# Block 0 of an in-projection: first casts interleaved by quarters, raw weights in x's raw buffers, rotation's sum on VectorE

## The chip, the cores and the metric

One core of one Trainium2 chip runs the kernel, with its engines TensorE (PE; its weight loads are shown as PEld), VectorE (DVE), ScalarE (ACT), GpSimd (POOL) and SyncE (SP, whose queue, SPq, issues the transfers). The metric is device microseconds of one execution, the median of several runs; lower is better.

## The reference

One layer of a hybrid encoder over 2048 prompt tokens and 8 x 16 sample tokens, all in float32. Cut to what matters here:

```python
def trunk_layer(x, pos, ..., w_in, ...):
    qm, km, vm, om, ip, fp, qa, ka, va = split_in(x @ w_in)
    km = km.reshape(B, T, M_HEADS, M_HEAD_DIM) * (M_HEAD_DIM ** -0.5)
    ...
    hm, C1, n1, m1 = mlstm_chunkwise(qm, km, vm, logi, logf, C0, n0, m0, mchunk)
    og = jax.nn.sigmoid(om)
    qa = rope(qa.reshape(B, T, A_Q_HEADS, A_HEAD_DIM), pos)
    ka = rope(ka.reshape(B, T, A_KV_HEADS, A_HEAD_DIM), pos)
    ha = swa_prompt(qa, ka, va, attn_sinks)      # or swa_step for the sample tokens
    mix = jnp.concatenate([hm, ha], axis=-1) @ w_out
    h = layer_norm(DEEPNORM_ALPHA * x + mix, ln1_g, ln1_b)
    f, conv_rows = conv_ffn(h, conv_prev, w_up, w_conv, b_conv, w_down)
    return layer_norm(DEEPNORM_ALPHA * h + f, ln2_g, ln2_b), ...

def rope(x, pos):
    ...
    return jnp.concatenate([x1 * cos - x2 * sin, x2 * cos + x1 * sin], axis=-1)
```

Only `x @ w_in` for the first 512 prompt tokens and the sample tokens (block 0), and the rotation of `qa` there, are touched by the change.

## The kernel before

**Stages.** The in-projection runs over four blocks of tokens (`IBLOCKS`; block 0 is tokens 0 to 511 and the 128 sample tokens, called the batch). After it, and partly woven into it, come the mLSTM and attention chains, the out-projection, and the ConvFFN.

**Products.** The wide part of `w_in` is cut into five groups of 512 columns (`NG`; groups 0 and 1 are q and k, 2 is qa with the rotation, 3 the output gate with a tanh, 4 is v). Each group is multiplied by a block of x as 2 x 2 quadrants in seven half-size products instead of eight, called steps 1, 2, 7, 6, 5, 4, 3 here; "product 3.5" is group 3, step 5. Steps 1, 2, 3, 4 and 5 use a quadrant of the weight itself or one with a difference in it, steps 7 and 6 sums and differences made in place in the raw weights by DVE (`split_first`, L516, L518, L521, L537). The products accumulate in three PSUM banks A, B, C (`self.ib`, shown as dps): steps 1 and 2 in A, 6, 5 and 3 in B, 7 and 4 in C (L722). A product is 24 matmuls of 128x256; in block 0 steps 1, 2, 5 and 4 have 12 more for the batch (L744, bank psx).

**Operands.** Every float32 operand is split into a rounded part and a remainder: ACT casts the high part (L220 for weights, L580 for x), DVE subtracts it for the low part (L221, L581). TensorE multiplies high x high, high x low and low x high.

**Order of block 0.** `i_begin` writes the order down: products 0.1, 0.2, 1.1, then the narrow gate-and-key tiles (L748, weights `wg`), then 0.7, 0.6, 0.5, 0.4, 0.3, 1.7; then for each group g: g.6, g.2, g.5, (g+1).1, g.4, g.3, (g+1).7; the last group ends 4.6, 4.2, 4.5, 4.3, 4.4. A list of units in the same order says what is loaded (`next_raw`, L429) and split (`next_split`, L475). `advance` runs both as far ahead as room allows: the split weights lie in a ring of four units, so a split waits for the product four units back; the raw weights lie in four slots taken in turn (`raw_slot`, tag wraw), and the next load waits until the oldest slot's weight is used for the last time (`raw_free`, L415). A group loads four raw quadrants, at its steps 1 (a11), 7 (a21), 6 (a22) and 2 (a12). a11 is done after the split of step 2, a21 after that of step 5, a22 after 4, a12 after 3.

Groups 2 to 4 write the split weights of steps 6, 5, 7 and 3 to memory for the later blocks (L533); x's four raw quadrants of a block lie in buffers xr1 to xr4 (`x_load`, L549).

**After a product** (`i_after`, L798): step 6 copies B out (L801), step 5 copies B (L801) and adds C (L807), step 4 adds C to step 6's copy (L807), steps 2 and 3 copy A and B out (L793, or the tanh at L790), step 3 also copies A to B (L829). For group 2 each result is then rotated (`rope`, L888): two products into a buffer rb, one in place (L900) and a sum (L901) that POOL does, for the batch too (`i_batch`); then SP stores it (L783, L840).

**Start.** SP loads x's first quadrant and the first weight in halves, in turn. `split_first` casts and subtracts the weight in four quarters, `x_steps` those of x in four quarters (L576 to L581).

The instructions of each engine run in the order in which a scheduler put them, except that TensorE's order is the program's.

Of the kernel before, what the change touches and what calls it, by code (L numbers as in the profile page):

```python
# [14 lines left out]
P = 128  # L15
# [31 lines left out]
HT = 2 * P  # L47
# [157 lines left out]
class Prog:  # L205
# [137 lines left out]
    def i_begin(self):  # L343
# [40 lines left out]
        self.halves = [0, 0]  # L384
        self.raws = []
        self.raw_of = {}
        self.xn = self.ny = 0
        self.hs = {}
        self.spare = False
# [39 lines left out]
    def next_raw(self):  # L429
# [4 lines left out]

        there = u[0] == "p" and u[1] == 0 and (u[2] == 0 and u[3] != 1 or u[3] in (5, 4, 3) or u[2:] == (1, 1))
        there = there or u[:2] == ("g", -1)
        if not there and not self.kept(u) and not self.raw_free():
            return False
        self.ur += 1
        if u[0] == "p":  # L440
            _, b, g, s = u
            quad = {1: (0, 0), 2: (0, 1), 7: (1, 0), 6: (1, 1), 4: (1, 1)}
            if b == 0:

                if s in (5, 4, 3):
                    return True
                if g == 0:
                    if s == 1:
                        self.i_first_weights()
                    return True  # L450
                if (g, s) == (1, 1):
                    e = self.raw_of[g, quad[s]] = [self.tp.tile([P, 4, HT], F32, name="wraw", tag="qk", bufs=2), False]
                    nc.sync.dma_start(e[0], a["wi"][g][quad[s]])
                    return True
                self.raw_of[g, quad[s]] = e = self.raw_slot([P, 4, HT])
                src = a["wi"][g][quad[s]]
            elif self.kept(u):
                return True
            else:
                self.raw_of[u] = e = self.raw_slot([P, 4, HT])  # L460
                src = a["wi"][g][quad[s]] if s in (1, 2, 4) else self.zws[g][SUMS.index(s)][0]
# [43 lines left out]
    def split_first(self, g, s, hi, lo):  # L505
# [19 lines left out]
        q = {1: a11, 7: a11, 6: a11, 2: a12, 3: a12, 5: a21, 4: a22}[s]  # L525
        n = 4 if (g, s) == (0, 1) else 1
        f = r[q].rearrange("p a b -> p (a b)")
        for i in range(n):
            c = slice(i * 1024 // n, (i + 1) * 1024 // n)
            self.split(hi[:, c], lo[:, c], f[:, c])  # L530
        if g >= KEPT and s in SUMS:
            for i, t in enumerate((hi, lo)):
                nc.sync.dma_start(self.zws[g][SUMS.index(s)][i].rearrange("p a b -> p (a b)"), t.bitcast(F32))  # L533
# [20 lines left out]
    def x_steps(self, b, *steps):  # L554
# [3 lines left out]
        for s in steps:  # L558
# [4 lines left out]
            elif s == "t2":  # L563

                V.tensor_add(self.xt[0], self.xt[0], r(1))
            elif s == "t4":

                V.tensor_sub(r(4), r(3), self.xt[0])
                self.xt[1] = True
            elif s == "t1":  # L570

                V.tensor_sub(r(2), r(2), r(1))
            else:
                x = self.xt[0] if s in (7, 6) else r({1: 1, 2: 3, 3: 4, "b12": 2, 5: 2, 4: 4}[s])

                self.hx[b, s] = h, l = self.x_slot(4 if s == "b12" else s)  # L576
                n = 4 if (b, s) == (0, 1) else 1
                for i in range(n):
                    k = slice(i * 4 // n, (i + 1) * 4 // n)
                    nc.scalar.copy(h[:, k], x[:, k])  # L580
                    V.tensor_sub(l[:, k], x[:, k], h[:, k].bitcast(F32))  # L581

    def x_single(self, *steps):

# [15 lines left out]
    def i_dense(self):  # L600
# [26 lines left out]
        self.rope_load(IBLOCKS[0][2], 2)  # L627
        self.rope_load(NPT, 1)
        self.next_split()
        self.x_steps(0, 1)  # L630
        self.x_single(1)
        self.next_split()
        self.x_steps(0, 2)
# [10 lines left out]
        for item in self.items:  # L644
# [9 lines left out]
            if item[0] == "t":  # L654
# [14 lines left out]
                elif ti == 3 and b or ti == 4:  # L669
                    self.release(4)  # L670
                elif item in begin:
                    self.x_steps(0, *begin[item])
                if ti == 3 and b or ti == 4:
                    self.x_steps(b, 4)
                    if b:
                        self.x_steps(b, 5)
# [108 lines left out]
    def i_out(self, b, g, i, j, src):  # L785
# [6 lines left out]
        elif not i:  # L792
            nc.scalar.copy(ev, src)  # L793
        if g == 2:
            self.rope(ev, IBLOCKS[b][2 * j], 2, nc.gpsimd)
        self.i_store(b, g, i, j, ev)

    def i_after(self, b, g, s):  # L798
# [32 lines left out]
    def i_batch(self, g):  # L831
# [4 lines left out]
        ev = self.zev()  # L836
        if g == 2:
            nc.scalar.copy(ev, ps)
            self.rope(ev, t, 1, nc.gpsimd)
            nc.sync.dma_start(self.zqa[t], ev)  # L840
            return
        if g < 2:
# [1333 lines left out]
```

## Time and profile before

| what | value |
|---|---|
| median of 3 runs | 2326.87 us (2325.21 to 2328.39) |
| the profiled execution | 2326.59 us |
| its span, first to last instruction | 2324.8 us |
| granted TensorE clock, mean | 0.996 |
| block 0 of the in-projection | about the first 163 us |

Times in rows count from the span's start. A timeline row is start, duration, engine, line, operation, output<-input, shape, count, and in brackets how long the engine was idle before and what released it. A chain row is start, duration and what. A wait row is who waited for whom: us in total, times, longest. A window row is the stretch, its length, busy us (and instructions) of PE, PEld, DVE, ACT and POOL, the granted clock of TensorE, the busy share of the DMA engines, and GB/s. A row of groups is line, engine, operation, operands, count, busy us, mean ns of one, and idle time before. A row of transfers has the count, KB each, and median us from issue to landing.

### The profile page before, as it was taken

The page shows a single profiled execution, that of the slowest core. Times are in us where ns is not written, and L with a number is a line of the kernel's source. Part 1 is how long each engine was busy: PE and PEld are TensorE (multiplying, and loading weights), DVE is VectorE, ACT ScalarE, POOL GpSimd, SP SyncE. Part 2 cuts the span into 40 slices and gives each one's busy share as a digit, 9 for nine tenths or more (in the row PEclk, how much of TensorE's full clock was granted, in tenths as well). Part 3 has the DMA queues.
Part 4 walks back from the last instruction along what each step waited for, and adds up shares of the span by engine and source line. Part 5 has one row for each costly group of instructions (what it writes and reads, how often), then busy time and mean ns, then how long its engine had stood idle before and what let it go on. Part 6 is the DMA issues. An engine that isn't in the chain of part 4 may idle for free.

```text
span 2324.8 us, 39933 instructions
## 1 busy us (share of the span) xinstructions
PE 2282.6 (98%) x14425; PEld 2104.6 (91%) x14425; DVE 1801.6 (77%) x3148; ACT 1304.3 (56%) x2465; POOL 244.3 (11%) x298
## 2 busy tenths in 40 slices
PE   9989999999999999999999999999999999999998
PEld 8989988899987777999999999999999988888887
DVE  8677586787678888987888766778766787796897
ACT  5353466676666665655556455556555644554653
POOL 0101101101111221300002000002000000000100
PEclk9999999999999999999999999999999999999999
DMA  7888889889977667787776899887998886756753
GB/s 275 276 309 287 284 294 328 292 279 330 307 254 259 210 212 242 262 321 283 287 272 252 273 319 323 307 309 264 324 298 265 246 284 224 244 197 216 244 189 109
DMA packets 297365, 624.98 MB, mean 269 GB/s; under 512 B 47052, under 2 KB 140240, under 8 KB 297168
## 3 DMA queue, kind: packets, MB, share of 16 engines
q1 hardware_dynamic: 296304, 619.29, 77.8%
q10 hardware_dynamic: 864, 3.15, 0.4%
q8 instruction: 114, 1.87, 0.3%
q14 instruction: 83, 0.68, 0.1%
HBM read 451.78 MB, written 170.56 MB: 268 GB/s over the span
## 4 chain that ended last, share of the span: by engine, by line
PE 78%; DVE 7%; DMA 4%; ACT 2%; issue 2%; SPq 0%; POOL 0%; DVEq 0%; ACTq 0%; POOLq 0%
PE dps L1880 18%; PE fup L1880 18%; PE dps L735 11%; PE dps L2084 6%; PE fht L2084 5%; PE fup L2084 5%; PE dps L225 2%; PE dps L760 2%; PE dps L227 1%; PE dps L226 1%; PE ppo L1371 1%; DVE w L221 1%; PE psc L1322 1%; DMA txy<-wdn 1%; PE ppt L1365 1%
## 5 line engine op out<-in xcount | busy, mean ns | idle before, releaser
L1880 PE MATMUL dps<-hh,uw 128*128 128x384 f32 (+1 forms) x1848 | 477.5, 327 | 5.3 <-DVE u L1913 2.6
L1880 PE MATMUL fup<-hh,uw 128*128 128x384 f32 (+1 forms) x1848 | 476.5, 326 | 0.0
L1928 DVE SCALAR_TENSOR_TENSOR cc<-u,cw,cc 128x768 f32<-128x768 f32 (+1 forms) x264 | 257.8, 978 | 125.1 <-ACT cc L1926 121.7
L1880 PEld LDWEIGHTS dps<-hh,uw 128*128 128x128 f32 x1848 | 329.4, 188 | 7.6 <-DVE u L1913 3.2
L1880 PEld LDWEIGHTS fup<-hh,uw 128*128 128x128 f32 x1848 | 329.4, 188 | 0.0
L1880 PE MATMUL fup<-hl,uw 128*128 128x384 f32 (+1 forms) x924 | 301.3, 326 | 1.1 <-DVE hl L221 1.1
L1880 PE MATMUL dps<-hl,uw 128*128 128x384 f32 (+1 forms) x924 | 301.0, 326 | 0.0
L735 PE MATMUL dps<-w,oh 128*128 128x256 f32 x1344 | 253.4, 284 | 10.1 <-ACT zev L801 5.4
L221 DVE TENSOR_TENSOR w<-wraw,w 128x1024 fp32r<-128x1024 f32 (+2 forms) x163 | 187.9, 1158 | 61.9 <-ACT w L220 59.5
L735 PEld LDWEIGHTS dps<-w,oh 128*128 128x128 f32 x1344 | 211.4, 190 | 23.1 <-issue 9.8
L220 ACT CAST w<-wraw 128x1024 fp32r<-128x1024 f32 (+2 forms) x163 | 161.1, 995 | 124.4 <-PE dps L735 52.2
L220 ACT CAST uw<-wraw 128x1024 fp32r<-128x1024 f32 x126 | 123.3, 982 | 173.7 <-PE dps L2084 104.2
L221 DVE TENSOR_TENSOR uw<-wraw,uw 128x1024 fp32r<-128x1024 f32 x126 | 142.6, 1132 | 63.9 <-ACT uw L220 63.8
L735 PE MATMUL dps<-w,ol 128*128 128x256 f32 x672 | 187.3, 279 | 0.0
L1926 ACT ACTIVATE cc<-u,cw 128x768 f32<-128x768 f32 (+1 forms) x132 | 132.0, 1000 | 96.5 <-DVE u L1922 93.3
L735 PE MATMUL dps<-oh,w 128*128 128x256 f32 x896 | 171.4, 285 | 4.9 <-ACT oh L580 1.7
L1880 PEld LDWEIGHTS fup<-hl,uw 128*128 128x128 f32 x924 | 173.5, 188 | 1.9 <-DVE hl L221 1.9
L1880 PEld LDWEIGHTS dps<-hl,uw 128*128 128x128 f32 x924 | 173.5, 188 | 0.0
L2084 PE MATMUL fup<-uw,fu 128*128 128x512 f32 x726 | 169.0, 389 | 0.0
L2084 PEld LDWEIGHTS fup<-uw,fu 128*128 128x128 f32 x726 | 136.2, 188 | 28.2
L2084 PE MATMUL dps<-uw,fu 128*128 128x512 f32 x660 | 161.0, 389 | 0.1
L735 PEld LDWEIGHTS dps<-oh,w 128*128 128x128 f32 x896 | 141.3, 189 | 11.0 <-issue 4.1
(336 smaller groups left out, 4601.0 us busy)
## 6 DMA issues: line engine op xcount, KB each, us to landing
uw<-zw SPq DMA_DIRECT2D x176, 512.0 KB, 5.1
zw<-uw SPq DMA_DIRECT2D x88, 512.0 KB, 2.9
w<-zws SPq DMA_DIRECT2D x72, 512.0 KB, 6.5
wv<-wup SPq DMA_DIRECT2D x66, 512.0 KB, 6.0
wraw<-wi SPq DMA_DIRECT2D x64, 512.0 KB, 5.0
wraw<-zt SPq DMA_DIRECT2D x60, 512.0 KB, 4.5
wraw<-wdn SPq DMA_DIRECT2D x45, 512.0 KB, 3.8
wraw<-wo SPq DMA_DIRECT2D x40, 512.0 KB, 4.7
```

Of the source, the lines that this page charges most:

```text
L220: nc.scalar.copy(hi, src)
L221: nc.vector.tensor_sub(lo, src, hi.bitcast(F32))
L225: mm(out, ah, bh, start=start, stop=False)
L226: mm(out, ah, bl, start=False, stop=False)
L227: mm(out, al, bh, start=False, stop=stop)
L735: mm(o, l, r, start=s in (1, 7) and c == k == i == 0, stop=k == 3 and i == 2, skip_group_check=True)
L760: mm(o, x, w, start=k == i == 0, stop=k == KD - 1 and i == 2, skip_group_check=True)
L1322: nc.tensor.matmul(ps[kvh][:, j, :nk], q[rs, j0 + j], k[rs, sel], start=i == 0, stop=i == 2)
L1880: mm(ps, l[:, k], r[:, k], start=s in (1, 7) and k == 0 and i == 0, stop=k == 3 and i == 2, skip_group_check=True)
L1926: S.activation(c[:, v], u[:, v, 2:2 + n], AF.Identity, bias=w[3], scale=w[2])
L1928: V.scalar_tensor_tensor(c[:, v], u[:, v, i:i + n], w[i], c[:, v], op0=ALU.mult, op1=ALU.add)
L2084: mm(ps, l[:, k, c], r[:, k], start=s in (1, 4, 7) and u == 0 and k == 0 and i == 0, stop=u == nu - 1 and k == n - 1 and i == 2, skip_grou ...
```

## The change

Three edits in block 0; what is computed stays the same.

1. The eight casts of x's first quadrant and the first weight (a quarter each), and their subtractions, are written as one sequence: x, x, w, w, w, x, w, x, each cast issued after the one before. Before, x's and w's were written apart.
2. Two entries `x_room` let the weights of group 3 for steps 1 and 7 live in x's raw buffers xr1 and xr3, once x of block 0 has been used there (after tile 2), and skip the test for a free slot. x of block 1 goes into the same buffers afterwards.
3. In block 0 the rotation's sum is added by DVE, not POOL.

```diff
+        self.x_room = {1: [None, False], 7: [None, False]}
...
+        room = self.x_room.get(u[3]) if u[0] == "p" and u[1:3] in ((0, 1), (0, 3)) else None
+        there = there or room is not None and room[1]
         if not there and not self.kept(u) and not self.raw_free():
             return False
...
-                self.raw_of[g, quad[s]] = e = self.raw_slot([P, 4, HT])
+                if room and room[1]:
+                    e = self.x_room[s] = [self.x_raw(1 if s == 1 else 3), False]
+                else:
+                    e = self.raw_slot([P, 4, HT])
+                self.raw_of[g, quad[s]] = e
                 src = a["wi"][g][quad[s]]
...
-        for i in range(n):
-            c = slice(i * 1024 // n, (i + 1) * 1024 // n)
-            self.split(hi[:, c], lo[:, c], f[:, c])
+        if n > 1:
+            x = self.xr[0, 1]
+            xh, xl = self.hx[0, 1] = self.x_slot(1)
+            fv, hv, lv = [t.rearrange("p (a b) -> p a b", a=4) for t in (f, hi, lo)]
+            after = None
+            for h, l, src, k in ((xh, xl, x, 0), (xh, xl, x, 1), (hv, lv, fv, 0), (hv, lv, fv, 1),
+                                 (hv, lv, fv, 2), (xh, xl, x, 2), (hv, lv, fv, 3), (xh, xl, x, 3)):
+                with self.tc.issue_after(after) if after else nullcontext():
+                    after = nc.scalar.copy(h[:, k], src[:, k]).ins
+                V.tensor_sub(l[:, k], src[:, k], h[:, k].bitcast(F32))
+        else:
+            self.split(hi, lo, f)
...
-                n = 4 if (b, s) == (0, 1) else 1
-                for i in range(n):
-                    k = slice(i * 4 // n, (i + 1) * 4 // n)
-                    nc.scalar.copy(h[:, k], x[:, k])
-                    V.tensor_sub(l[:, k], x[:, k], h[:, k].bitcast(F32))
+                nc.scalar.copy(h, x)
+                V.tensor_sub(l, x, h.bitcast(F32))
...
-        self.x_steps(0, 1)
...
+                    for e in self.x_room.values() if ti == 2 else ():
+                        e[1] = True
...
-            self.rope(ev, IBLOCKS[b][2 * j], 2, nc.gpsimd)
+            self.rope(ev, IBLOCKS[b][2 * j], 2, nc.gpsimd if b else nc.vector)
...
-            self.rope(ev, t, 1, nc.gpsimd)
+            self.rope(ev, t, 1, nc.vector)
```

What it moves, at three places. First, ACT at the start (xr is x's quadrant, wraw the raw weight, oh and w their high parts; dps<-dps is the copy of A to B after product 0.1). Before:

```order
L580 COPY oh<-xr 128x256
L220 COPY w<-wraw 128x256 x4
L580 COPY oh<-xr 128x256 x3
L592 COPY xs<-xsr 128x512
L220 COPY w<-wraw 128x1024
L580 COPY oh<-xr 128x1024
L592 COPY xs<-xsr 128x512
L809 COPY dps<-dps 128x512
```

Now:

```order
L543 COPY oh<-xr 128x256 x2
L543 COPY w<-wraw 128x256 x3
L543 COPY oh<-xr 128x256
L543 COPY w<-wraw 128x256
L543 COPY oh<-xr 128x256
L605 COPY xs<-xsr 128x512
L220 COPY w<-wraw 128x1024
L823 COPY dps<-dps 128x512
L593 COPY oh<-xr 128x1024
```

x's second quarter stands ahead of all weights, and the copy of A to B has moved ahead of the cast of x's next quadrant. DVE's subtractions follow the same order.

Second, ACT around products 3.6 and 3.5 (numbers are buffers; w_1530, w_1562, w_1592 and w_1639 are the weights of 3.5, 4.1, 3.4 and 3.3; zev_1590 is B copied out after 3.6, zev_1683 after 3.5). Before:

```order
L220 COPY w_1530<-wraw_1224 128x1024
L793 COPY zev_1520<-dps_250 128x512
L829 COPY dps_250<-dps_249 128x512
L220 COPY w_1562<-wraw_1494 128x1024
L801 COPY zev_1590<-dps_250 128x512
L220 COPY w_1592<-wraw_1284 128x1024
L790 ACTIVATE zev_1634<-dps_249 128x512
L220 COPY w_1639<-wraw_1337 128x1024
L801 COPY zev_1683<-dps_250 128x512
```

Now (w_1532 is 3.5's):

```order
L220 COPY w_1532<-xr_1043 128x1024
L807 COPY zev_1522<-dps_250 128x512
L843 COPY dps_250<-dps_249 128x512
L220 COPY w_1562<-wraw_1288 128x1024
L220 COPY w_1592<-wraw_1183 128x1024
L815 COPY zev_1590<-dps_250 128x512
L804 ACTIVATE zev_1634<-dps_249 128x512
L220 COPY w_1639<-wraw_1228 128x1024
L815 COPY zev_1683<-dps_250 128x512
```

The casts for 4.1 and 3.4 both stand ahead of the copy of B now. On DVE, group 3's first operations on the raw weights (xr_1041 is a11, xr_1043 a21, wraw_1183 a22) come ahead of the split of product 2.4 (w_1285):

```order
L221 TENSOR_TENSOR w_1255<-xr_1041,w_1254 128x1024
L528 TENSOR_TENSOR xr_1041<-xr_1041,xr_1043 128x1024
L523 TENSOR_TENSOR xr_1043<-xr_1043,wraw_1183 128x1024
L221 TENSOR_TENSOR w_1285<-wraw_994,w_1284 128x1024
L912 TENSOR_TENSOR rb_1328<-zev_1326,ropet_296 128x8x32
L913 TENSOR_TENSOR rb_1328<-zev_1326,ropet_296 128x8x32
L914 TENSOR_TENSOR zev_1326<-zev_1326,ropet_296 128x512
L915 TENSOR_TENSOR zev_1326<-zev_1326,rb_1328 128x512
```

Before, the work of the second and third row (L521, L516) stood behind that split, and the last row's was POOL's.

Third, SP's queue after group 2. wraw_1494, wraw_1536 and wraw_1596 are group 4's raw weights for steps 1, 7 and 6. Before:

```order
L783 DMA zqa1_127<-zev_1278 128x256
L906 DMA ropet_1862<-rope 128x192
L1429 DMA cns_2650<-cn0 128x1032
L462 DMA wraw_1494<-wi 128x1024
L840 DMA zqa16_142<-zev_1481 128x512
L533 DMA zws3_1_85<-w_1530 128x1024
L783 DMA zqa2_128<-zev_1520 128x256
L783 DMA zqa3_129<-zev_1520 128x256
L533 DMA zws3_1_85<-w_1531 128x1024
L462 DMA wraw_1536<-wi 128x1024
L462 DMA wraw_1596<-wi 128x1024
```

Now, the same piece of the queue (the loads for steps 1 and 7, wraw_1288 and wraw_1341, stand 13 and 8 rows above its first row; xr_1734 and xr_1738 are x of block 1):

```order
L797 DMA zqa1_127<-zev_1282 128x256
L920 DMA ropet_1862<-rope 128x192
L1443 DMA cns_2650<-cn0 128x1032
L549 DMA zws3_1_85<-w_1532 128x1024
L549 DMA zws3_1_85<-w_1533 128x1024
L854 DMA zqa16_142<-zev_1485 128x512
L568 DMA xr_1734<-xq 128x1024
L568 DMA xr_1738<-xq 128x1024
L469 DMA wraw_1596<-wi 128x1024
L797 DMA zqa2_128<-zev_1522 128x256
```

Of group 4's three loads only the one for step 6 is still here, behind the batch's store and two loads of x. The two loads of x stood about 60 rows further up before, where the loads of xr_1041 and xr_1043 stand now.

## The prediction

> **What bounds the kernel now.** I read the page first: busy shares, then the chain that ended last.
>
> ```profile
> PE 2282.6 (98%) x14425; PEld 2104.6 (91%) x14425; DVE 1801.6 (77%) x3148; ACT 1304.3 (56%) x2465; POOL 244.3 (11%) x298
> PE 78%; DVE 7%; DMA 4%; ACT 2%; issue 2%; SPq 0%; POOL 0%; DVEq 0%; ACTq 0%; POOLq 0%
> ```
>
> TensorE is busy 98% of the span, so this change can only win what TensorE loses inside block 0, and a half-clock stretch counts as busy. The waits of PE, asked for 60 to 170 us, and the timeline of ACT, SP, POOL and DVE around the first of them:
>
> ```profile
> PE dps L735 <- ACT zev L801: 4.0, 2, 2.3
> PE dps L760 <- DVE ol L581: 2.7, 1, 2.7
> 115.59 1.56 PE L744 MATMUL psx<-w,xs 128*128 128x256 f32 x12
> 119.47 0.39 PE L735 MATMUL dps<-w,oh 128*128 128x256 f32 x1 [2.32 <-ACT zev L801]
> 109.12 0.57 ACT L829 COPY dps<-dps 128x512 f32<-128x512 f32 x1
> 117.89 1.04 ACT L220 CAST w<-wraw 128x1024 fp32r<-128x1024 f32 x1 [8.19 <-DMA wraw<-wi]
> 118.84 0.58 ACT L801 COPY zev<-dps 128x512 f32<-128x512 f32 x1
> 112.80 0.38 SPq L462 DMA_DIRECT2D wraw<-wi  x1
> 109.88 0.80 SPq L783 DMA_DIRECT2D zqa<-zev  x2
> 107.65 2.21 POOL L901 TENSOR_TENSOR zev<-zev,rb 128x512 f32<-128x512 f32 x1 [3.54 <-DVE zev L900]
> 110.57 1.22 DVE L537 TENSOR_TENSOR wraw<-wraw 128x1024 f32<-128x1024 f32 x1
> ```
>
> From bottom to top this is one story. The slot for group 4's first raw weight comes free with the subtraction at L537 (ends 111.79). Its load is issued at 112.80, behind a store that POOL released at 109.86, and arrives about 5.1 us later. ACT has the cast of that weight (117.89) at the head of its queue, idle 8.19 us, and behind it the evacuation of bank B (118.84). Product 3.5 writes B, so PE stops from 117.15 (115.59 + 1.56) to 119.47, although its own weights were ready.
>
> The stop costs more than itself. The chain gives the products behind it, and the 1-us windows the clock:
>
> ```profile
> 119.47 4.61 PE dps L735 x24
> 125.48 2.72 PE dps L735 x24
> 128.20 1.40 PE psx L744 x12
> 122.00:123.00 1.00, 1.00 (x6) 1.00 (x6) 1.00 (x1) 0.00 (x0) 0.00 (x0) 0.50 0.93 270
> 124.00:125.00 1.00, 1.00 (x11) 1.00 (x10) 0.51 (x1) 0.59 (x1) 0.00 (x0) 1.00 0.92 337
> ```
>
> The same 24 matmuls take 4.61 us after the stop and 2.72 one product later: 1.89 us lost at a granted clock of 0.50. So the stop is worth 2.32 + 1.89 = 4.21 us.
>
> **The change, part by part.**
>
> *Two more homes for raw weights.* Group 3's weights for its steps 1 and 7 go to x's buffers and are loaded where x of block 1 was loaded before, same bytes, same places in SP's queue (the first two rows). Group 4's first weight then needs the slot of group 2's step 4, which is free when this split ends:
>
> ```profile
> 37.49 0.34 SPq L552 DMA_DIRECT2D xr<-xq  x1
> 40.35 0.42 SPq L552 DMA_DIRECT2D xr<-xq  x1
> 89.38 1.23 DVE L221 TENSOR_TENSOR w<-wraw,w 128x1024 fp32r<-128x1024 f32 x1 [0.42 <-ACT w L220]
> wraw<-wi SPq DMA_DIRECT2D x7, 512.0 KB, 5.3
> ```
>
> 90.6 us; DVE now does two other 1.2-us operations first (the first ones of group 3's steps 7 and 6, in the order shown with the change), so about 92 to 93, plus 5.3 us of median time to landing: 98. The cast's other condition is the release of its ring places by product 3.7, about 110.3 (back from 117.15: 3.2 with its batch part 4.12, 3.6 without 2.72). It has 12 us to spare. In the new order of ACT the cast of step 3.4 also stands ahead of the evacuation; it waits for product 3.6, which ends at 117.15 - 4.12 = 113.0, exactly what the evacuation waits for too. So 1.05 us of cast, then 0.58: done by 114.7, PE needs it at 117.15. The stop goes, with 2.4 us to spare: **4.21 us gained**. That is the lower bound of the wait too: if the half clock stays or returns elsewhere, only 2.32.
>
> *Rotation's sum on VectorE.* Five sums leave POOL in block 0.
>
> ```profile
> L901 POOL TENSOR_TENSOR zev<-zev,rb 128x512 f32<-128x512 f32 x17 | 28.0, 1649 | 148.9 <-DVE zev L900 136.0 <-DVE amx L1330 7.8 <-issue 2.7
> L900 DVE TENSOR_TENSOR zev<-zev,ropet 128x512 f32<-128x512 f32 x5 | 3.4, 687 | 0.1
> 100.00:110.00 10.00, 10.00 (x90) 10.00 (x89) 7.48 (x11) 4.70 (x6) 4.42 (x2) 1.00 0.83 302
> ```
>
> The nearest row for the sum on DVE is the rotation's product of the same shape, 0.687 us: 5 x 0.687 = 3.4 us more on DVE between 92 and 118, where it is busy 7.48 of 10 us. POOL's took up to 2.21, and DVE waited for POOL before the next rotation (one buffer rb), so DVE gains back about what it pays. Behind each sum on DVE stand a split or the sum that frees bank C; the tightest is the latter for product 2.4. Back from 117.15 by the chain's lengths (3.2: 4.12; 3.6, 3.7 and 2.3: 2.72 each; 2.4's batch part: 1.40), C is complete at 103.5, its sum done 0.7 later, and product 3.7 wants C at 107.6. The cover is 3.4 us, so the edit costs nothing; without cover it would cost at most 0.7 a sum. Value taken: 0, since the stores it frees on SP no longer stand before a load that matters.
>
> *First casts by quarters.* The start before:
>
> ```profile
> 7.50 0.71 ACT L220 CAST w<-wraw 128x256 fp32r<-128x256 f32 x2 [1.79 <-DMA wraw<-wi]
> 8.12 1.01 ACT L580 CAST oh<-xr 128x256 fp32r<-128x256 f32 x3
> 8.57 0.39 PE L735 MATMUL dps<-oh,w 128*128 128x256 f32 x1 [1.75 <-ACT oh L580]
> 12.37 2.29 PE L744 MATMUL psx<-w,xs 128*128 128x256 f32 x12
> 14.50 0.28 PE L735 MATMUL dps<-oh,w 128*128 128x256 f32 x1
> 11.39 1.04 ACT L580 CAST oh<-xr 128x1024 fp32r<-128x1024 f32 x1 [0.27 <-DMA xr<-xq]
> 12.47 1.23 DVE L581 TENSOR_TENSOR ol<-xr,oh 128x1024 fp32r<-128x1024 f32 x1
> 11.00:12.00 1.00, 1.00 (x7) 1.00 (x6) 0.84 (x1) 0.73 (x2) 0.00 (x0) 0.50 1.03 409
> ```
>
> x's second quarter sat in memory but its cast stood behind the weights' second half (7.50). Now it is cast at 4.4, so 12 matmuls can run before that half lands instead of 3, and the first product ends about 1.6 us sooner. But the second product needs x's next quarter: its load lands at 11.39, cast 1.04, remainder 1.23, so 13.70, whatever happened before; and ACT now has the copy of bank A to B (0.58) ahead of that cast. It cannot go on before about 13.8, against 14.50 now (its second matmul 14.62): at best 0.7 us gained. The other end is a new idle time of 1.8 us before it: if that earns a half-clock stretch, as the 1.75 us at 8.57 did (clock 0.50 at 11), the second product (2.72) pays up to 1.7, and the net is a loss of 0.9. I take 0.
>
> *What is late next.* Group 4's loads also come sooner. Later stop, and what led to it:
>
> ```profile
> 124.49 1.23 DVE L521 TENSOR_TENSOR wraw<-wraw 128x1024 f32<-128x1024 f32 x1 [1.40 <-DMA wraw<-wi]
> 127.39 1.23 DVE L516 TENSOR_TENSOR wraw<-wraw 128x1024 f32<-128x1024 f32 x1 [1.67 <-DMA wraw<-wi]
> 140.68 0.79 SPq L783 DMA_DIRECT2D zog<-zev  x2
> 143.81 6.87 DMA wraw<-wg
> 150.76 0.63 ACT L220 CAST w<-wraw 128x528 fp32r<-128x528 f32 x1 [2.91 <-DMA wraw<-wg]
> 151.93 0.38 PE L735 MATMUL dps<-w,oh 128*128 128x256 f32 x1 [1.66 <-ACT zev L801]
> ```
>
> DVE waited twice for group 4's raw weights, fell behind, released the store at 140.68 late, and behind that store stood the load of the gates' weights; its cast stood ahead of PE's evacuation once more. Group 4's step-7 weight is now far ahead, its step-6 weight about 1.2 us earlier against PE (landing near 122, PE's products 4.21 earlier: 14.5 us before product 4.6 ends now, 15.7 then). If that lead reaches the gates' load whole, the stop of 1.66 falls by about 1; below 0.6 it cannot go, since product 4.3 writes the bank that 4.5 has just filled and an evacuation takes 0.58. Bounds 0 and 1.0; I take 0.7, nearer the whole, since DVE has hardly any gap in that stretch in which a lead would be lost. The 2.7 us at L760 hang on casts behind product 4.4 and stay.
>
> Sum: 2.32 + 1.89 + 0 + 0 + 0.7 = 4.9 us. The profiled execution took 2326.59 (span 2324.8 and 1.8 around), 0.3 under the median of 2326.87. 2326.59 - 4.9 = **2321.7 us**, 0.22% under the median. No other order changes: TensorE's row for row, and the other engines' from block 0's last group on.
>
> [...]
>
> **The rivals.**
>
> *The half clock is not saved but moves.* A loss of 1.89 at half speed is a stretch of some 3.8 us, and what earns it may be how an idle time falls in such a stretch. All of block 0 behind the stop shifts by 4 us, so another idle time (1.66 at 151.93, or the new one at 13 us) can earn one. For it: the stop of 1.66 earned none, though the one of 1.75 at 8.57 did:
>
> ```profile
> 153.00:154.00 1.00, 1.00 (x11) 1.00 (x11) 0.34 (x1) 0.63 (x1) 0.00 (x0) 1.00 0.88 193
> ```
>
> Against: the 1.66 shrinks. Gain 4.9 - 1.9 = 3.0: 2323.6 us.
>
> *The lead carries on.* The gates' load brings the next block's first weight forward too, and part of the 2.7 us at L760 goes with a stretch of half clock that follows it: another 1 to 2.5 us. Against: that wait hangs on casts of x. 2320 us.
>
> *The stop stays.* ACT's evacuation has two casts ahead of it instead of one; if either weight is still late, nothing is won but the start's parts: 2326.5.
>
> *Slower: the load of group 4's step-6 weight.* On SP it now stands behind the batch's store and two x loads, and its slot is freed by a DVE split at about 117. DVE's sum for it (1.23) is ahead of the sum that frees bank C (0.69) in DVE's order, and product 3.4 wants C at 117.15 + 2 x 4.12 = 125.4. So it must land by 123.5, 6.5 us after issue; each us later stops PE a us. The gain of 4.9 is eaten at a landing of 128.4, slower by 0.2% at 133. With 2.5 MB ahead and with it (two x loads, two stores, itself) at the 337 GB/s of the window it takes 7.4 us, a loss of 0.9; only with twice that does it get slower: landing at 134, 2332 us.
>
> **How the numbers follow.** A measurement of this kernel tells 0.2% (4.65 us) from no change: faster is below 2322.2, slower above 2331.5. Forecast 0.58, its own range 2320 to 2323.5 (start -0.7 to 0.9, the later stop 0 to 1), 0.50 of it counted as faster and 0.08 as the same. Moved clock 0.17, same. Lead carries on 0.13, faster. Stop stays 0.05, same. Slower rival 0.07. Faster 0.63, same 0.30, slower 0.07. For eight in ten I leave out the slower rival and the far end of the carried lead: 2318.5 to 2326.8.
>
> **What would show it.** Right: no PE wait on the evacuation near 117, ACT's cast there waiting for PE instead of DMA, clock 1.00 through 113 to 123, the load of group 4's first weight issued before 95, no sums on POOL until block 1. The start: second product's second matmul at 13.8, clock of 12 to 18 us telling which end. The later stop: under 1.2 us. Wrong: a PE wait before product 3.4 on a DVE sum behind L523 (the load), ACT waiting for a DMA before 117, or the same stops with the whole time unmoved.

## The result, and the profile after

| kernel | median of runs | ratio to the kernel before |
|---|---|---|
| before | 2328.57 us (22 runs, 2325.21 to 2339.74) | 1 |
| changed | 2323.67 us (22 runs, 2317.85 to 2328.43) | 0.9973, 95% interval 0.9966 to 0.9981 |

The ratio is a gain of 6.3 us (4.4 to 7.9) of 2328.57, and the mean times have the same ratio. The two medians differ by less, 4.90 us (a ratio of 0.9979), so the size of the gain is uncertain by more than 1 us even between these two ways to take it. The profiled execution of the changed kernel took 2325.43 us, with a span of 2323.7: only 1.1 us less than the one of before. Both numbers are explained below.

The page of the changed kernel, busy shares and the chain that ended last:

```profile
PE 2285.4 (98%) x14425; PEld 2105.5 (91%) x14425; DVE 1803.5 (78%) x3153; ACT 1304.1 (56%) x2465; POOL 223.5 (10%) x293
PE 70%; DVE 7%; ACT 3%; issue 3%; DMA 3%; POOL 0%; SPq 0%; DVEq 0%; ACTq 0%; POOLq 0%
```

Five instructions have gone from POOL to DVE. PE is busy 2.8 us longer although it runs the same 14425 matmuls. Part of that is time at half clock: 17.1 us of this execution before its last matmul and 13.7 us of the one of before passed at a clock of 0.50 (the stretches in the last section), and PE counts as busy there (3.42 of the 3.42 us from 10.53 on, before). The waits of PE from 60 to 170 us, where before the stop of 2.3 and one of 1.66 stood:

```profile
PE dps L774 <- DVE ol L594: 2.7, 1, 2.7
PE dps L774 <- ACT oh L593: 0.4, 1, 0.4
```

Only the wait before block 1's first tile is left. The place of the first stop, in the timelines of PE, ACT, SP and DVE (L469 is the load, L220 the casts, L815 the copy of bank B):

```profile
115.17 1.56 PE L758 MATMUL psx<-w,xs 128*128 128x256 f32 x12
116.57 0.28 PE L749 MATMUL dps<-w,oh 128*128 128x256 f32 x1
112.53 1.05 ACT L220 CAST w<-wraw 128x1024 fp32r<-128x1024 f32 x1 [1.66 <-PE dps L749]
113.49 0.57 ACT L815 COPY zev<-dps 128x512 f32<-128x512 f32 x1
91.14 0.33 SPq L469 DMA_DIRECT2D wraw<-wi  x1
116.00 0.33 SPq L469 DMA_DIRECT2D wraw<-wi  x1
120.53 1.23 DVE L523 TENSOR_TENSOR wraw<-wraw 128x1024 f32<-128x1024 f32 x1 [1.56 <-DMA wraw<-wi]
113.00:123.00 10.00, 10.00 (x90) 10.00 (x89) 7.61 (x10) 4.97 (x7) 0.00 (x0) 1.00 1.01 353
```

Product 3.5 follows the batch part at once, and the clock is 1.00 in the whole stretch (last row). ACT waits for PE there, no longer for a DMA, and copies B by 114.06. Group 4's first weight goes out at 91.14 instead of 112.80; its step-6 weight goes out at 116.00 and DVE uses it at 120.53, 3 us before the limit of 123.5 that the slower rival set.

The place of the later stop. Only the loads of the gates and the two rows of ACT remain of it, and PE does not wait:

```profile
137.62 1.24 SPq L476 DMA_DIRECT2D wraw<-wg  x1
144.22 0.63 ACT L220 CAST w<-wraw 128x528 fp32r<-128x528 f32 x1 [1.17 <-DMA wraw<-wg]
144.76 0.58 ACT L815 COPY zev<-dps 128x512 f32<-128x512 f32 x1
```

The end of block 0, PE before and after:

```profile
159.46 0.51 PE L760 MATMUL dps<-w,oh 128*128 128x264 f32 x2 [0.40 <-ACT oh L580]
162.64 0.39 PE L760 MATMUL dps<-w,ol 128*128 128x264 f32 x1 [2.68 <-DVE ol L581]
```
```profile
152.99 0.51 PE L774 MATMUL dps<-w,oh 128*128 128x264 f32 x2 [0.45 <-ACT oh L593]
156.18 0.59 PE L774 MATMUL dps<-w,ol 128*128 128x264 f32 x1 [2.67 <-DVE ol L594]
```

The same matmul starts 6.47 us earlier (159.46 - 152.99; 6.67 and 6.63 in experiments 4 and 9 below, which hold the same two edits). So a lead of the size of the whole gain is there at the end of block 0. In this one execution most of it was lost again. The windows (clock is the column after the count of POOL), before and after:

```profile
160.00:170.00 10.00, 7.36 (x48) 7.36 (x49) 7.42 (x9) 4.41 (x8) 0.00 (x0) 0.83 0.81 272
900.00:910.00 10.00, 10.00 (x47) 8.10 (x46) 10.00 (x16) 2.62 (x3) 0.06 (x1) 1.00 0.88 311
1590.00:1600.00 10.00, 8.29 (x54) 8.02 (x53) 10.00 (x12) 7.06 (x11) 7.99 (x3) 1.00 0.61 202
```
```profile
150.00:160.00 10.00, 6.88 (x41) 6.46 (x41) 8.09 (x8) 5.41 (x7) 0.00 (x0) 0.74 0.88 295
160.00:170.00 10.00, 10.00 (x80) 10.00 (x79) 7.07 (x13) 5.26 (x9) 0.00 (x0) 0.92 0.78 261
900.00:910.00 10.00, 8.45 (x34) 6.20 (x33) 10.00 (x17) 1.55 (x3) 1.70 (x2) 0.83 0.71 266
1590.00:1600.00 10.00, 9.52 (x52) 9.52 (x53) 10.00 (x11) 4.34 (x8) 4.87 (x3) 0.83 0.49 156
```

Behind block 1's first tile the clock was 0.50 twice as long as before (6.83 us in place of 3.41; the lead falls from 6.47 to 5.60 us there), and at 906 and 1592 us, where nothing was changed, there were stretches of half clock that the other execution did not have. The last section lists the waits ahead of them.

### The profile page after: what moved, and what is told of

Its sections match the earlier page's. It is cut to its first block, busy times and chain, and to the rows that moved or that the text cites. A ratio compares the mean times of both kernels' runs of the same rounds, so it can differ in the third digit from the quotient of the medians.

```text
span 2323.7 us, 39928 instructions
## 1 busy us (share of the span) xinstructions
PE 2285.4 (98%) x14425; PEld 2105.5 (91%) x14425; DVE 1803.5 (78%) x3153; ACT 1304.1 (56%) x2465; POOL 223.5 (10%) x293
## 4 chain that ended last, share of the span: by engine, by line
PE 70%; DVE 7%; ACT 3%; issue 3%; DMA 3%; POOL 0%; SPq 0%; DVEq 0%; ACTq 0%; POOLq 0%
PE fup L1894 18%; PE dps L1894 18%; PE dps L2098 6%; PE fht L2098 5%; PE fup L2098 5%; PE dps L749 5%; PE dps L225 2%; PE dps L227 2%; PE dps L226 2%; PE ppo L1385 1%; DVE w L221 1%; PE psc L1336 1%; DVE uw L221 1%; PE dps L774 1%; PE ppt L1379 1%
## 5 line engine op out<-in xcount | busy, mean ns | idle before, releaser
L221 DVE TENSOR_TENSOR w<-wraw,w 128x1024 fp32r<-128x1024 f32 (+1 forms) x155 | 181.5, 1175 | 52.8 <-ACT w L220 52.0
L220 ACT CAST uw<-wraw 128x1024 fp32r<-128x1024 f32 x126 | 123.2, 981 | 173.4 <-PE dps L2098 104.1
L220 ACT CAST w<-wraw 128x1024 fp32r<-128x1024 f32 (+1 forms) x155 | 155.5, 1009 | 111.8 <-PE dps L749 60.9
```

The source lines that it names most:

```text
L220: nc.scalar.copy(hi, src)
L221: nc.vector.tensor_sub(lo, src, hi.bitcast(F32))
```

## The experiments

All ratios are to the kernel before, from 5 rounds in four sessions, each on one chip; medians of before in those sessions were 2326.94 (experiments 1 to 4), 2327.73 (5 to 8), 2327.92 (9 to 11) and 2329.15 us (12). Each kernel ran 12 times, but 11 times in experiment 3, 6 in 4 and 5 in 7. "Lead" is how much earlier a matmul starts than the same matmul of the kernel before.

**1. First casts alone.** Off the changed kernel:

```diff
-        self.x_room = {1: [None, False], 7: [None, False]}
+        self.x_room = {}
-            self.rope(ev, IBLOCKS[b][2 * j], 2, nc.gpsimd if b else nc.vector)
+            self.rope(ev, IBLOCKS[b][2 * j], 2, nc.gpsimd)
-            self.rope(ev, t, 1, nc.vector)
+            self.rope(ev, t, 1, nc.gpsimd)
```

> Only the first casts by quarters, no extra homes, sums on POOL. Theory (the homes do the work, the casts next to nothing): the second product goes on about 1 us earlier than before, some of it is lost again by the wait on DVE near 49 us, so 0.4 us earlier at 100 us; the stop of 2.32 us near 117 and the later one of 1.66 are both there; ratio 0.9998, within 0.2% of before. Rival (the casts carry the gain): 1 us or more still there at 100 us and the later stops shorter; ratio 0.9985 or less.

Ratio 1.0001 (0.999 to 1.0013): nothing, as the theory had it. Its way there was another: the lead at 100 us was 1.41 us and not 0.4, and the later stop of 1.66 did not occur. The start came sooner, and the stop was longer, with its half clock (PE, and the window around it):

```profile
118.66 0.58 PE L749 MATMUL dps<-w,oh 128*128 128x256 f32 x1 [2.92 <-ACT zev L815]
113.00:123.00 10.00, 7.08 (x44) 6.88 (x44) 5.83 (x8) 3.92 (x5) 1.29 (x1) 0.75 0.93 312
```

The lead of 1.41 was 0.81 behind the stop, and -0.31 at 139 us. The clock of 0.75 is half clock for 5.0 of these 10 us, and the matmuls stay slow past them (the batch part at 123.95 takes 1.94 us in place of 1.56), where the kernel before has 3.41 us at 0.50.

**2. Homes alone.** The casts of before, the sums on POOL, `x_room` as changed.

> Only the two extra homes, casts as before, sums on POOL. Theory: load of group 4's first weight issued before 95 us, no PE wait on B's evacuation near 117 (4.2 us gained with its half clock), later stop of 1.66 gone or under 0.5: 5 to 6 us earlier at the first tile of block 1, ratio 0.9975. Rival (the stores held up by POOL were the cause, so the sum does it): stop near 117 still over 1.5 us, ratio 0.9995 or more.

Ratio 0.9997 (0.9984 to 1.0011). The stop at 117 is gone, as the theory had it, but the ratio is the rival's, and two waits stand behind the place. PE, SP, DVE and POOL:

```profile
126.02 0.39 PE L744 MATMUL dps<-w,oh 128*128 128x256 f32 x1 [1.45 <-DVE zev L816]
148.53 0.39 PE L744 MATMUL dps<-w,oh 128*128 128x256 f32 x1 [1.51 <-ACT zev L810]
116.25 0.80 SPq L792 DMA_DIRECT2D zqa<-zev  x2
117.10 0.44 SPq L559 DMA_DIRECT2D xr<-xq  x1
118.47 0.33 SPq L469 DMA_DIRECT2D wraw<-wi  x1
112.45 0.42 DVE L907 TENSOR_TENSOR rb<-zev,ropet 128x256 f32<-128x256 f32 x1 [1.18 <-POOL zev L910]
115.11 2.20 DVE L528 TENSOR_TENSOR wraw<-wraw 128x1024 f32<-128x1024 f32 x1
117.23 1.22 DVE L221 TENSOR_TENSOR w<-wraw,w 128x1024 fp32r<-128x1024 f32 x1
124.14 1.22 DVE L523 TENSOR_TENSOR wraw<-wraw 128x1024 f32<-128x1024 f32 x1 [4.22 <-DMA wraw<-wi]
114.08 2.14 POOL L910 TENSOR_TENSOR zev<-zev,rb 128x512 f32<-128x512 f32 x1 [1.67 <-DVE zev L909]
```

This is the prediction's slower rival, at its place: the step-6 load of group 4 goes out at 118.47, when the split that frees its slot has ended (117.23 + 1.22), behind a store that POOL's sum held and an x load; DVE waits 4.22 us for it, and PE waits before product 3.4. It costs 1.45, not the whole gain. In the trace the same matmul of product 3.4 still comes 3.4 us earlier than before (129.43 there); a time with an interval of 3 us either way cannot confirm that.

**3. Sum on VectorE alone.** `x_room = {}`, the casts of before.

> Only the rotation's sum on DVE, casts and homes as before. Theory (the homes do it): the load of group 4's first weight still waits for its slot, freed on DVE; without POOL's sums that comes some 2 us sooner (issue near 110.5 instead of 112.8), so the stop near 117 shrinks to between 0 and 1 us but the loads for steps 7 and 6 stay late and the later stop stays over 1.2: ratio 0.998 to 0.9995. Rival (the sum does all): both stops gone, ratio 0.9975. Second rival (it does nothing): issue within 0.5 us of 112.8, ratio 1.000.

Ratio 0.9994 (0.9982 to 1.0006), within the theory's range, and so are the traces. The load of group 4's first weight leaves SP at 110.40 instead of 112.80, and ACT has copied B by 117.82. SP, ACT, PE's wait at the later stop, and the window:

```profile
110.40 0.33 SPq L469 DMA_DIRECT2D wraw<-wi  x1
116.28 1.05 ACT L220 CAST w<-wraw 128x1024 fp32r<-128x1024 f32 x1 [5.92 <-DMA wraw<-wi]
149.50 0.39 PE L744 MATMUL dps<-w,oh 128*128 128x256 f32 x1 [1.76 <-ACT zev L810]
113.00:123.00 10.00, 9.95 (x87) 9.75 (x86) 7.05 (x9) 4.77 (x7) 0.00 (x0) 1.00 0.87 296
```

PE does not wait near 117 in this execution, whose products ran 0.7 us later than before from 50 us on (50.11 for 49.44); without that, up to 0.7 of the stop would be left, if the load did not come sooner too. The half clock is gone with it (1.00 in the window), but the later wait (1.76) stays. So in the trace the sum alone also takes most of the first stop away, and the time does not show it.

**4. Homes and sum, without the casts.**

> Homes and sum, casts as before. Theory: everything of the change but 0.4 us, first tile of block 1 about 6 us earlier than before, ratio 0.9975. Rival (the casts matter): under 5 us earlier, ratio 0.998 or more.

Ratio 0.997 (0.9959 to 0.9981), as for the whole change, and block 1's first tile is 6.67 us earlier, both as the theory had it. Neither homes nor sum alone reaches the ratio: their intervals begin at 0.9984 and 0.9982, just above its end. SP and DVE here:

```profile
115.54 0.33 SPq L469 DMA_DIRECT2D wraw<-wi  x1
112.56 1.22 DVE L528 TENSOR_TENSOR wraw<-wraw 128x1024 f32<-128x1024 f32 x1
```

The same operation L528 that took 2.20 us beside POOL's sum takes 1.22, and starts 2.55 sooner. The load is out 2.93 sooner than with the homes alone, while TensorE's product 3.5 stands at the same time in both (within 0.05 us).

**5, 6, 12. How do the sums on POOL spoil the homes?** Homes alone, with the stores of rotated tiles issued from POOL's queue (5), with two buffers rb (6), and with both (12):

```diff
-            nc.sync.dma_start(self.zqa[t], ev)
+            nc.gpsimd.dma_start(self.zqa[t], ev)
...
-        B = self.mp.tile([P, 512], F32, name="rb", tag="rb", bufs=1)[:, :n]
+        B = self.mp.tile([P, 512], F32, name="rb", tag="rb", bufs=2)[:, :n]
```

> Homes only, with the rotation's sums left on POOL as before and the first casts as before, but block 0's six stores of rotated tiles issued from POOL's own queue instead of SP's. It tells apart two ways in which the sums on POOL spoil the homes. Theory A: the harm is on SP, which stands at a store that POOL's sum releases, so that the load of group 4's step-6 weight goes out late (118.5 us in the homes-only run against 116.0 in the changed kernel). Then that load goes out by 116.5 here, PE's wait of 1.45 us at 126 is gone, and the time is 2.5 to 4 us below the kernel before. Theory B: the harm is on DVE, which waits for POOL's sums and is slowed to 2.2 us an operation beside them, so the slot's split itself is late. Then the load still goes out after 117.5, a wait of 1 us or more stands near 126, and the time is within 2 us of the kernel before.

> Homes only, sums left on POOL and stores on SP, but the rotation's buffer rb doubled, so that DVE's next rotation need not wait for POOL's sum. Theory A (SP held by the store that waits for POOL's sum): the load of group 4's step-6 weight still goes out at about 118, the wait near 126 stays at 1 us or more, time within 2 us of the kernel before. Theory B (DVE waiting for POOL through rb): the split that frees the slot ends by 116.5, the load goes out by 117, the wait near 126 falls under 0.5, time 2 to 4 us below the kernel before. A third reading, DVE operations blocked whole while a sum runs on POOL: operations of 2.2 us on DVE beside POOL's sums stay in this run whatever the buffers are.

> Homes only, the sums left on POOL, with both remedies at once: the stores of rotated tiles issued from POOL's queue and the rotation's buffer doubled. Theory (the sum on VectorE is worth what SP's hold and the wait through rb cost together): PE waits neither 1 us near 126 nor 1 us near 148 us, ratio to the kernel before 0.9965 to 0.9975, as for homes and sum together (0.997). Rival (a third cost stays: VectorE's operations that stand whole behind a sum on POOL, 2.2 us in place of 1.2): operations of 2.2 us on VectorE remain, the waits are as in the run with the other queue alone (0.9 near 148), ratio 0.998.

| kernel | ratio (interval) | step-6 load, against the 19th matmul of product 3.5 | PE's wait near 126 | near 148 |
|---|---|---|---|---|
| homes alone | 0.9997 (0.9984 to 1.0011) | +0.27 us | 1.5 | 1.5 |
| with POOL's queue | 0.998 (0.997 to 0.999) | +0.27 | none | 0.9 |
| with two rb | 0.9999 (0.9989 to 1.001) | -0.29 | 0.7 | 1.9 |
| with both | 0.9991 (0.9977 to 1.0005) | -0.28 | 0.2 | 0.7 |
| homes and sum on DVE | 0.997 (0.9959 to 0.9981) | -2.61 | none | none |

The starts of that matmul are 118.20, 119.45, 122.36, 122.12 and 118.15 us; the kernels differ there by what happened in the first 55 us, so the load is told against that matmul. Theory A of experiment 5 fails in its own observable: the load did not go out sooner when SP was free. Its consequence came all the same, it seems by another way: with SP free, x's loads went out at 110.81 and 112.92, where with the homes alone one of them went right ahead of this load (117.10), and DVE had the weight 4.05 us after the issue instead of 5.67. Theory B of experiment 6 fails too: with two buffers DVE no longer waits for rb, but its operations elsewhere take longer beside POOL's sums (two of 0.42 us take 1.52 and 1.51). In experiment 12 the waits are small, as its theory had them, but operations of 2.2 us stay, as its rival had it, and the ratio 0.9991 is that of neither. DVE and POOL there:

```profile
114.06 1.51 DVE L908 TENSOR_TENSOR rb<-zev,ropet 128x256 f32<-128x256 f32 x1
115.49 1.21 DVE L221 TENSOR_TENSOR w<-xr,w 128x1024 fp32r<-128x1024 f32 x1
118.48 2.20 DVE L528 TENSOR_TENSOR wraw<-wraw 128x1024 f32<-128x1024 f32 x1
117.45 2.14 POOL L910 TENSOR_TENSOR zev<-zev,rb 128x512 f32<-128x512 f32 x1 [1.31 <-ACT w L220]
```

What the third reading looked for is there: behind the start of a sum on POOL (113.94 and 117.45), an operation of 0.42 takes 1.51 and one of 1.22 takes 2.20. With the sum on DVE the second takes 1.22 (experiment 4), and only the sum on DVE moves the load by more than 0.6 us.

The ratios of 6 and 12 do not price the two buffers, since these two kernels lose time at another place. With two rb the narrow tiles' rotations stand elsewhere on DVE, DVE waits there for a load, and TensorE waits 2.90 us (6) and 2.35 (12) near 51 us where it waited 0.91 with the homes alone. From 55 us on they stand 3.3 and 3.1 us behind the kernel before. From there to product 4.3 (151.93 before) the lead grows by 2.6 us with the homes alone, 4.6 in experiment 5, 3.0 in 6, 4.5 in 12, and 6.2 with the sum on DVE. So by the traces the other queue recovers about half of what the sum does. In time, 5 is clear of 1 (its interval ends at 0.999), and its interval overlaps those of the homes alone and of homes and sum.

**7. The batch's cast first.** Changed kernel with one item moved:

```diff
-            3: [3, "t4"], 4: ["b12", "t1"]},
+            3: [3], 4: ["b12", "t4", "t1"]},
```

> The changed kernel with one item of the order of the last group of block 0 moved: the cast for step 4 of x of block 1 stands behind the cast of the batch part instead of ahead of it. My prediction said that the 2.7 us before block 1's first tile hang on these casts. If so, the remainder on DVE for the tile that PE waits for comes one cast and one subtraction sooner (about 1.2 us), PE's wait falls from 2.67 to about 1.45, and with fewer idle microseconds a half-clock stretch there may be shorter or gone: 1 to 3 us below the changed kernel, ratio to the kernel before 0.9960 to 0.9970. Rival: the wait hangs on the end of TensorE's own product 4.4 through buffers; then the wait stays at 2.7 and the time at the changed kernel's (ratio 0.997 to 0.998).

The wait hangs on DVE's remainder behind that item, as expected:

```profile
153.80 0.39 PE L774 MATMUL dps<-w,ol 128*128 128x264 f32 x1 [1.54 <-DVE ol L594]
160.00:170.00 10.00, 10.00 (x87) 10.00 (x87) 6.72 (x11) 4.95 (x8) 0.00 (x0) 1.00 0.94 335
```

1.54 in place of 2.67, and no half clock behind it: 1.00 from 150 to 160 us too. Ratio 0.9968 (0.9956 to 0.998): 1.2 us below the changed kernel by the two ratios, which overlapping intervals of 5 and 22 runs do not prove.

**8. The gap filled.** Changed kernel with 26 matmuls before the first tile of block 1, whose result the tile overwrites:

```diff
+        if (b, ti) == (1, 2):
+            f = self.hx[1, 1][0]
+            for k in range(26):
+                mm(ps[:, :HT], f[:, k % 4, :P], f[:, k % 4], start=True, stop=True, ...)
```

> The changed kernel with 26 extra matmuls (128x256) whose result the next product overwrites, put before block 1's first tile, where PE idles 0.45 and 2.67 us. It does more work than the kernel needs and writes nothing else. Theory (the idle time earns the half-clock stretch that the changed kernel's profile has at 154.7 us): no stretch at half clock between 150 and 170 us, the next tile's matmuls at full speed, 1.7 to 3.4 us below the changed kernel, ratio to the kernel before 0.9955 to 0.9968. Rival (the stretches fall where they like and idle time has no part in it): stretches in number and length as before somewhere in the first 300 us, time equal to the changed kernel's within 1 us or up to 0.5 us longer (ratio 0.997 to 0.998).

```profile
152.24 3.27 PE L768 MATMUL dps<-oh 128*128 128x256 f32 x26
155.93 0.39 PE L778 MATMUL dps<-w,ol 128*128 128x264 f32 x1 [0.17 <-DVE ol L594]
160.00:170.00 10.00, 10.00 (x87) 10.00 (x86) 7.94 (x14) 5.53 (x8) 0.00 (x0) 1.00 0.98 339
```

No half clock from 150 to 170 us, as the theory has it (1.00 from 150 to 160 us too). The time does not show it: 0.9979 (0.9968 to 0.999), that of the changed kernel, as the rival has it.

**9. x's next quarter by quarters.** `n = 4 if (b, s) == (0, 2) else 1` for cast and subtraction at L593 of the changed kernel.

> The changed kernel with x's next quarter (for step 2 of product 0.2, line 593) also cast and subtracted by quarters. My prediction said that nothing can be won at the start before 13.8 us, since product 0.2's whole cast and remainder stand there. Theory (the start's win is taken back at 49 us, where VectorE is late): product 0.2's second matmul comes about 1 us sooner than 13.56, PE's wait at 49 us grows from 1.46 by about as much, and from 50 us on the lead over the changed kernel is under 0.3 us; ratio to the kernel before 0.9965 to 0.998 as for the changed kernel. Rival (the start is on the path of the end): the lead of about 1 us is still there behind 50 us, time 1 us below the changed kernel.

Product 0.2's second matmul comes 0.88 sooner (12.68 for 13.56). The theory named the wrong place: at 49 the wait stays (1.49 us), and the lead over the changed kernel passes it (0.86 behind it). It ends at block 1's first tile (152.83 for 152.99). ACT there, changed kernel and this one:

```profile
149.51 1.05 ACT L220 CAST w<-wraw 128x1024 fp32r<-128x1024 f32 x1 [1.99 <-DMA wraw<-wi]
```
```profile
149.35 1.05 ACT L220 CAST w<-wraw 128x1024 fp32r<-128x1024 f32 x1 [2.64 <-DMA wraw<-wi]
```

Both wait for the same load, and 0.16 us of the lead is left. Ratio 0.9967 (0.9952 to 0.9981).

**10 and 11. The moved cast without the first casts, and with the quarters of 9.**

> The kernel before plus the two homes and the sum on VectorE plus the moved cast for step 4 of the next block, with the start's casts as in the kernel before. Theory (the first casts are worth nothing): the time of the kernel with the casts and the same moved cast, 2319.6 against 2327.7 before, ratio 0.996 to 0.9975; PE's wait before block 1's first tile 1.5 us. Rival (the casts give the 0.4 to 1.1 us by which the first products came sooner in the changed kernel's trace): ratio 0.0002 to 0.0005 higher.

> A version meant to beat both kernels: the changed kernel with the moved cast for step 4 of the next block and x's next quarter cast by quarters. Theory (a stretch at half clock of 3.41 us follows where PE has been idle for more than about half of such a stretch, and the shortened wait of 1.5 us is below that): no half-clock stretch between 150 and 170 us, ratio to the kernel before 0.9955 to 0.997. Rival (idle time has no part in it): a half-clock stretch there as in the changed kernel's profile, ratio 0.997 to 0.998.

Without the first casts: 0.998 (0.9966 to 0.9993), above the range of its theory. With the quarters: 0.997 (0.9958 to 0.9982), at the edge of its theory's range. The wait is 1.5 us and the clock 1.00 from 150 to 170 us in both. The first casts thus count for +0.0003 in one pair (changed kernel against 4) and -0.0012 in the other (7 against 10), neither beyond the intervals. No version is shown to beat the change: 7, 9 and 11 lie slightly below it, within the intervals.

## Why the prediction was right, and where not

The direction and the place were right: faster, with the whole lead made in block 0, and the median of 2323.67 lies within the range. The gain was 6.3 us by the ratio and 4.90 by the medians, where 4.9 was forecast. The forecast time of 2321.7 is 2.0 too low all the same, since it started from the three runs of before, whose median is 1.7 below that of the 22. It is chance that the median falls on the 2323.6 of the rival with the moved half clock: that rival has a gain of 3.0. Term by term, in the profiled execution:

- **The stop at 117, 2.32 + 1.89.** Right, with its mechanism: the lead was 0.42 us when the stop of before began and 4.62 when its half clock was over, 4.2 in all. The step-6 load was forecast for 117 and 122, and was 116.00 and 120.5.
- **The start, 0.** A lead of 1.06 at 13.56 (forecast: 13.8) without the feared half clock (1.00 in every microsecond from 9 to 18), 0.41 behind the wait at 49. Experiment 1 shows no gain from it without the other edits, and in 9 a further lead of this kind is lost at a load. It is also no larger than chance here: with the old casts, experiments 2, 3 and 4 stand at 0.82, -0.67 and 0.88 behind that wait. The choice of 0 stands.
- **The later stop, 0.7.** Mis-sized. It went whole: the lead grew from 4.75 to 6.54 there, 1.8 us. The step that failed is "below 0.6 it cannot go": bank B is complete after the 24 matmuls of product 4.5, and its batch part (1.40) runs while ACT copies B (0.58). The lead was a little larger too: the gates' load went out 6.19 us earlier (143.81 to 137.62), 1.44 ahead of TensorE, where about 1.2 was assumed.
- **The sum on VectorE, 0.** This step was wrong: "DVE gains back about what it pays", and "the stores it frees on SP no longer stand before a load that matters". The homes need the sum, or in part the other queue of experiment 5: with them alone, waits of 1.45 and 1.51 stand (experiment 2). The prediction counted the wait through rb and SP's store, and not that a DVE operation takes longer beside a sum on POOL, 2.20 us in place of 1.22. In experiment 2, from 98 to 118 us, DVE loses 2 x 0.98 in operations of 2.20 and 2 x 1.18 in waits; it pays three sums, which cost 0.60 each back to back: 4.3 - 1.8 = 2.5 of the 2.9 us by which the load moves.

The terms as they came, 4.2, 0.4 and 1.8, make 6.4 of the lead of 6.47. The forecast was still near, since the two edits were forecast together: the 2.4 us of cover that the prediction found for the stop, and the 3 us left to the step-6 load, are there because both edits were made. As a claim on the parts it was wrong: homes 4.21 and sum 0 were forecast. In the traces either edit alone takes the first stop away or nearly so, only both together leave no wait behind it before block 1, and in time neither alone was measurably anything.

One price in the slower rival does not come out of its own terms: twice 7.4 us from an issue at 117 lands at 132 and not at 134, which would give 2330 and not 2332 us.

**The rivals.** The stop did not stay. The slower rival was a real mechanism: it appears when the sum is left out. The lead did not carry on beyond block 0, as its own "against" said: the 2.7 us stayed, and experiment 7 moves them by the order of the casts. The moved half clock is seen in the profile (154.7 us, 6.83 long), but behind the same wait (2.67 and 2.68 us) one of 3.41 stood before, so only the difference was new in this execution.

## What to carry to other kernels

Cost edits that feed one chain together and apart: an early buffer is worth its price only if the engine that frees the next one keeps up, and here each edit alone was worth under 0.2%. When a small operation moves from GpSimd to VectorE, count also how much longer VectorE's operations take beside it (0.98 us more for two of them in experiment 2), not only what VectorE waits for by semaphore. Price an idle time of TensorE by its length, and look for the clock behind it: here waits of 1.75 and 2.32 us had 3.41 us at half clock behind them and one of 1.66 had none. One profiled execution of each kernel does not tell what such a stretch is worth on the mean of runs.

## What the runs showed of the hardware

**Operations of VectorE and GpSimd took longer beside each other.** In experiment 2, POOL's sum begins at 114.08 and DVE is busy until 115.08 (113.86 + 1.22); POOL ends at 116.22, 1.14 after that. DVE's next operation, begun at 115.11, takes 2.20 and ends at 117.31, 1.09 after POOL; with the sum on DVE the same operation takes 1.22 (experiment 4). In experiment 12 POOL's sum begins at 96.47 with DVE free, and takes 1.29, where the one at 114.08 took 2.14; the DVE operation begun at 96.60 takes 2.25. Operations of 2.20 for 1.22 are found in experiments 2, 5, 6 and 12, and of 1.51 for 0.42 in 6 and 12; the changed kernel has no sum on POOL and no DVE operation over 1.25 us from 90 to 124 us. The kernel before has no such DVE operation there either: its POOL sums take 2.15 to 2.22, and one takes 1.28.

**The waits with half clock behind them.** These are all waits of TensorE of 1.4 us or more behind its first product's start in the profiled executions of the two kernels, and the stretches at a clock of 0.50 at their ends:

| execution | wait ends at | us | clock 0.50 |
|---|---|---|---|
| before | 8.57 | 1.75 | 10.53 to 13.94 |
| before | 119.47 | 2.32 | 119.75 to 123.16 |
| before | 151.93 | 1.66 | none |
| before | 162.64 | 2.68 | 164.12 to 167.54 |
| before | 297.31 | 4.10 | 297.24 to 300.66 |
| before | 337.25 | 1.50 | none |
| before | 366.63 | 1.54 | none |
| before | 1593.60 | 1.71 | none |
| changed | 49.04 | 1.46 | none |
| changed | 156.18 | 2.67 | 154.72 to 161.54 |
| changed | 289.99 | 2.68 | 291.25 to 294.66 |
| changed | 359.77 | 1.52 | none |
| changed | 1590.48 | 1.75 | 1591.73 to 1595.14 |
| changed | 1859.83 | 1.45 | none |

In these two executions each of the five waits of 2.32 us and more has such a stretch, and of the nine of 1.45 to 1.75 us two have one, both of 1.75. One more stretch, at 905.65 in the changed kernel, has several shorter waits ahead of it: PE is busy 2.06 of the 3.60 us before it, and the longest wait is 1.24. A limit does not follow from this, also not that of about half of 3.41 us in the theory of experiment 11: in experiment 2 PE waits 2.7 us before block 1's first tile, around 158 us, and the clock is 1.00 from 148 to 168. Around that wait (2.1 to 2.7 us) the clock was below 1 in the executions of before (0.83 from 160 to 170 us), changed (0.74 from 150 to 160), 5, 6 and 12 (0.83, 0.83 and 0.66 from 158 to 168); in 7, 8, 10 and 11, where the wait was shortened or filled, it was 1.00 from 150 to 170.

This bears on the point at which the prediction was unsure: the wait of 1.75 us had a stretch behind it, and the one of 1.66 had none. The stop of 2.32 us had one, so the 1.89 us behind it were lost in this execution; what they are worth on the mean of runs was not shown. Nor was it shown what spreads the 22 runs of the changed kernel over 10 us (2317.85 to 2328.43) with the same order of work.
